# Four sums from GpSimd to VectorE, x loaded plainly for three row blocks, and one sum of weights made in DRAM

## The chip, the cores and the metric

The kernel runs on one core of a Trainium2 chip. The metric is the device time of one execution in microseconds (us); lower is better. Before the change the median of 3 runs was 624.9 us (624.47 to 625.27). The engines are called as the profile calls them: PE is TensorE's matrix product, PEld its loading of weights, DVE VectorE, ACT ScalarE, POOL GpSimd, SP the engine that only issues DMAs. DMAs issued by SP and by GpSimd share 16 DMA engines; only GpSimd's can add to what stands at the destination (accumulate).

## The reference: one decoder layer

For x of 512 rows and 1024 columns:

```python
h = x @ w_in                                  # ua, va, za, q, k, v, zb, ga, gb
ya = gelu(ua) * spatial(layer_norm(gelu(va))) * silu(za)      # branch A
yb = rms_norm(diff_attention(q, k, v)) * silu(zb)             # branch B
merged = sigmoid(ga) * (ya @ w_branch_a) + sigmoid(gb) * (yb @ w_branch_b)
mix_out = merged @ w_out
ple = sigmoid(x @ w_ple_gate) * (p @ w_ple)   # the embedding and its gate
x = layer_norm(ALPHA * x + mix_out + ple)     # ALPHA = 2 ** 0.25
```

All of it is float32.

## The kernel before

**Products.** Every float32 operand is split into a high half (a copy rounded by ScalarE: `wh`, `xh`, `xsh`) and a low half (the difference, a subtraction by VectorE: `wl`, `xl`, `xsl`). A product is three matmuls, high x high, high x low and low x high (`three`). The products of the embedding's gate and of branches A and B, like several before them, are *quads*: a product of two matrices cut into 2 x 2 blocks is made of seven block products instead of eight, as in Strassen's scheme. A quad needs sums of blocks of the left operand (for branch B: of `yb`; for branch A: of `ya`, which lies in the tile `ua`) and sums of blocks of the weights. It runs in seven steps. Each step has two units of weights of 128 x 1024 and 24 matmuls of 128 x 512, so a quad has 168.

**Weights.** A unit is loaded into a buffer `wr`, cut into halves, and used. Sums of weight blocks come in two ways. In the first (`follow`), GpSimd issues an accumulating DMA that adds the next block to the buffer as soon as VectorE has cut it (`wr<-in_w` on POOL). A chain of steps then shares a buffer, and each addition must land before ScalarE can cut the next unit. In the second (`make_sums`, tables `READY_MADE` and `PART_READY`), the sum is made in DRAM ahead of time: SP copies a block into `ws_...`, GpSimd adds another to it, and the step loads the finished sum like any other unit. `PART_READY` says which of the four sums are made so for each quad. From the gates on, eight buffers take the units in order; SP loads the next as soon as a buffer is free.

**Order.** All of the program is one list in order. `later(n, fn)` puts a piece of work n matmuls behind the present one; numbers like `YB_S2` or `GATES` are such distances from the start of a stage. This sets the order on each engine's queue. When an instruction then runs is up to its queue and its semaphores. SP's and GpSimd's queues are in order, too: a DMA that waits holds up all behind it.

**The stages that the change touches**, with their times in the profiled execution: the quad of the embedding's gate (433.5 to 477.5 us), the small product of p (to 488.7), branch B's quad (to 530.2), branch A's quad (to 572.7), and the output product (to 618.5). During the gate's quad the sums of `yb` for branch B's quad and two of those of `ya` are made. `combine` does it: with one number, VectorE makes the sum in one instruction of 128 x 4 x 256; with a pair of numbers, GpSimd makes it in two of half the size. In the gate's quad GpSimd makes four sums in eight instructions (L1235): `YB_S2` and `YB_N4` of `yb`, `YA_S1` and `YA_S3` of `ya`.

**The residual sum.** `embed` multiplies p's product by the gate and by 1/ALPHA into `base`. Then `residue` adds x to `base` by an accumulating DMA, one per block of 128 rows (L1287). In the output stage `fill` has ScalarE copy `base` times ALPHA into a PSUM bank (L1366), and the output product adds to that bank. So the bank ends as ALPHA x + ple + mix_out. VectorE takes statistics from the bank (`stats`, L1374) and normalises it (`last_norm`: L1380 for each bank, then L1384), and SP stores the block. The last block is done in three pieces instead of two.

**Gates.** The sigmoids of ga and gb were stored to DRAM. `load_gates` brings them back, two blocks at a time, into two places of the tile `gates` in turn.

Of the kernel before, what the change touches and what calls it, by code (L numbers as in the profile page):

```python
# [13 lines left out]
F32 = mybir.dt.float32  # L14
# [16 lines left out]
ALPHA = 2.0 ** 0.25  # L31
# [28 lines left out]
SILU = (20,)  # L60
CENTRE = (12, 24)
SPATIAL = (390, 32)
READY_MADE = {'va': (2, 6, 50, 32, 140, 174, 260, 314), 'wb': (162, 290, 170, 318, 356, 470), 'zq': (320, 430, 434, 538), 'ga': (540, 566), 'gb': (752, 786), 'pg': (612, 745)}
APART = 12
TABLES = (12, 40, 84)
TURN_K = (14, 18, 22, 24, 31, 36, 42)
# [25 lines left out]
FILL = ((14, 0, 1), (20, 2, 0), (24, 1, 1), (30, 3, 0), (136, 2, 1), (160, 3, 1), (164, 3, 2))  # L92
RETIRE = 8


# [40 lines left out]

READY = ("11", "21", 0, "22", 1, 2, 3)

PART_READY = {'zq': (0, 2), 'ga': (2,), 'gb': (2,), 'wb': (0, 1, 2), 'pg': (2,)}
KINDS = 'ycyyyyy'  # L140

MAKING = ((0, "begin", "11"), (2, "begin", "22"), (0, "add", "12"), (2, "add", "12"),
# [104 lines left out]
def hybrid_layer(ctx: ExitStack, tc: tile.TileContext, a, out: bass.AP):  # L247
    nc = tc.nc
    pe, dve, act, pool, sp = nc.tensor, nc.vector, nc.scalar, nc.gpsimd, nc.sync
# [5 lines left out]
    big = ctx.enter_context(tc.tile_pool(name="big", bufs=1))  # L255
# [6 lines left out]
    def pp():  # L262
        return pbank("pp", 3)
# [232 lines left out]
    def ask_xr(k):  # L496
# [14 lines left out]
                       base=0, pattern=[[-1, P]], channel_multiplier=1)  # L511
# [5 lines left out]
    cs = rp.tile([P, T], F32, name="cs")  # L517
# [132 lines left out]
    def quad(name, left, banks, place, done):  # L650

        X, Y, Z = banks
        if name == "zq":
            X, Y, Z = ([bank[:, :(2 - t) * 2 * P] for t, bank in enumerate(two)] for two in banks)
        kept = {}

        def keep(key, bank):
            kept[key] = tmp[0](key[0])[:, :bank.shape[-1]]  # L660
            act.activation(kept[key], bank, AF.Copy)  # L661

        def block(c, t, first, second, op, spare):
            z = place(c, t)
            z = spare if z is None else z
            dve.tensor_tensor(out=z, in0=first, in1=second, op=op)
            later(8 if name in SIGMOIDS else 2, done, c, t, z, z)

        goes_on = name in GOES_ON

        def after1(t):
            if goes_on:
                act.activation(X[t], Y[t], AF.Copy)
# [333 lines left out]
    sums.clear()  # L1007
    for name, at in READY_MADE.items():
        make_sums(name, at)
# [106 lines left out]
    va = post.tile([P, NT, D], F32, name="va", tag="V")  # L1116
# [142 lines left out]
    base = post.tile([P, NT, D], F32, name="base", tag="V")  # L1259
# [21 lines left out]

    def embed(c, t, bank):
        z = base[:, t, c * T:(c + 1) * T]
        dve.scalar_tensor_tensor(out=z, in0=bank, scalar=1.0 / ALPHA, in1=z, op0=OP.mult, op1=OP.mult)

    def residue(t):
        pool.dma_start(out=base[:, t, :], in_=a["x"][t * P:(t + 1) * P, :], accum_op=OP.add)  # L1287

    tx = pbank("tx", 1)
    banks = other_banks(), [tx, pp(), pp(), pp()]  # L1290
# [20 lines left out]
    pairs_of_gates = late.tile([P, 2, 2, T], F32, name="gates", tag="R")  # L1311

    def load_gates(name, c, t, i):
        two = pairs_of_gates[:, i]
        gate[name, c, t], gate[name, c, t + 1] = two[:, 0, :], two[:, 1, :]
        sp.dma_start(out=two, in_=gates[name][t:t + 2, c].rearrange("t p n -> p t n"))

    order = [(n, c, t) for n in ("gb", "ga") for c, t in ((0, 0), (1, 0), (1, 2), (0, 2))]
    for i, (n, what) in enumerate(zip(GATES, order)):
        later(n, load_gates, *what, i % 2)  # L1320
# [7 lines left out]
    for t, n in enumerate(RESIDUE):  # L1328
        later(n, residue, t)
    quad("wb", operands(xh, xl, ys, 0), pairs(True), place_b, mb_done)  # L1330

    norm_last = []
# [4 lines left out]

    later(LAST_NORM[0], load_last, "ln_g", "g")
    later(LAST_NORM[1], load_last, "ln_b", "b")

# [17 lines left out]
    last_columns = [[(0, T), (T, D)] for _ in range(NT - 1)] + [[(0, T), (T, T + T // 2), (T + T // 2, D)]]  # L1358
    held = {}

    def fill(t, i):
        c0, c1 = last_columns[t][i]
        bank = (pbank("sc", 2) if (t < 2 and i == 0) or (t >= 2 and i == 1) else
                pbank("tx", 1) if t == 2 else pp())
        held[t, i] = bank[:, :c1 - c0]
        act.activation(held[t, i], base[:, t, c0:c1], AF.Copy, scale=ALPHA)  # L1366

    for t in range(2):
        later(FIRST_FILL[t], fill, t, 0)
    quad("wa", of_ya, pairs(False), lambda c, t: None, merge)  # L1370


    def stats(t, piece, bank):
        dve.bn_stats(out=zst[t][:, piece, :], in_=bank)  # L1374

    def last_norm(t, cuts):
        mv, rs = rstd_of(zst[t])
        lg, lb = norm_last
        for i, cs in enumerate(slice(*c) for c in last_columns[t]):
            dve.scalar_tensor_tensor(out=base[:, t, cs], in0=held[t, i], scalar=mv[:, 0:1], in1=lg[:, cs],  # L1380
                                     op0=OP.subtract, op1=OP.mult)
# [86 lines left out]
```

## Time and profile before

| what | us |
|---|---|
| median of 3 runs | 624.9 |
| the profiled execution's own time | 627.2 |
| its span, first to last instruction | 625.5 |
| TensorE busy | 609.7 (97%) |
| VectorE busy | 465.1 (74%) |
| ScalarE busy | 341.6 (55%) |
| GpSimd busy | 133.8 (21%) |
| mean granted TensorE clock | 0.994 |

DMA moves 138.52 MB, 221 GB/s in the mean. A row of a timeline gives start and length of an instruction in us, its engine, its line, what it writes and reads, and in brackets how long the engine was idle before it and what ended the wait. A start that comes before the end of the row above shows pipelining. In a row of a window, the figure behind each engine is its busy time and the number of instructions; then come the granted clock, the mean busy share of the 16 DMA engines, and GB/s.

### The profile page before, as it was taken

What the parts mean: (1) busy time and instruction counts of PE and PEld (TensorE: products, weight loads), DVE (VectorE), ACT (ScalarE), POOL (GpSimd) and SP (SyncE); (2) the same over time, 40 slices, a digit from 0 to 9 for tenths busy, and PEclk for the clock granted to TensorE, in tenths of its full rate; (3) what the DMA queues carried; (4) which work ended last, traced back from release to release, by engine and by line L of the source; (5) the groups of instructions that cost most, each with busy time, mean ns of one, the idle gap of its engine ahead of it and who ended that gap; (6) DMA issues with size and microseconds to landing.
All of it is one profiled execution on the core that took longest, in us unless ns stands there. A gap on an engine that the chain in (4) does not pass through costs nothing.

```text
span 625.5 us, 8563 instructions
## 1 busy us (share of the span) xinstructions
PE 609.7 (97%) x3012; PEld 510.9 (82%) x3012; DVE 465.1 (74%) x769; ACT 341.6 (55%) x537; POOL 133.8 (21%) x144
## 2 busy tenths in 40 slices
PE   9999999999999999999999999999979998999995
PEld 6888888888888888888899888888858876787885
DVE  6995687878788775657578886677987686769465
ACT  6556664645644754578565656536745454545310
POOL 1234021332431630220102221141540111120000
PEclk9999999999999999999999999999999999999998
DMA  8689899678797696768989898968856887996002
GB/s 304 216 240 187 256 296 286 222 192 280 264 256 270 198 313 181 199 157 289 285 297 224 221 226 242 262 151 237 250 139 197 221 238 224 251 224 225 3 34 102
DMA packets 45631, 138.52 MB, mean 221 GB/s; under 512 B 6036, under 2 KB 7188, under 8 KB 45268
## 3 DMA queue, kind: packets, MB, share of 16 engines
q1 hardware_dynamic: 35092, 102.71, 45.9%
q0 software_dynamic: 9920, 34.87, 30.5%
q8 instruction: 24, 0.39, 0.3%
q10 hardware_dynamic: 576, 0.39, 0.2%
q14 instruction: 19, 0.16, 0.1%
HBM read 118.95 MB, written 30.54 MB: 239 GB/s over the span
## 4 chain that ended last, share of the span: by engine, by line
PE 84%; issue 5%; DMA 5%; DVE 4%; ACT 1%; POOL 0%; DVEq 0%; POOLq 0%; ACTq 0%; SPq 0%
PE ps_pp L281 50%; PE ps_sc L281 15%; PE ps_tx L281 7%; DMA wr<-in_w 3%; PE ps_sc L802 3%; PE ps_po L847 3%; DMA gates<-gate_gb 2%; PE ps_tr L836 1%; DVE wl L413 1%; PE ps_po L281 1%; PE ps_tr L281 1%; DVE xsl L1228 1%; PE ps_po L485 1%; PE ps_tr L1173 1%; PE ps_po L1173 1%
## 5 line engine op out<-in xcount | busy, mean ns | idle before, releaser
L413 DVE TENSOR_TENSOR wl<-wr,wh 128x1024 fp32r<-128x1024 f32 (+1 forms) x143 | 181.3, 1276 | 46.4 <-ACT wh L410 46.0
L410 ACT ACTIVATE wh<-wr 128x1024 fp32r<-128x1024 f32 (+1 forms) x143 | 146.1, 1032 | 73.9 <-DMA wr<-in_w 18.6
L281 PE MATMUL ps_pp<-xh,wh 128*128 128x512 f32 (+1 forms) x276 | 109.8, 399 | 0.0
L281 PE MATMUL ps_pp<-xl,wh 128*128 128x512 f32 (+1 forms) x276 | 107.3, 389 | 0.0
L281 PE MATMUL ps_pp<-xh,wl 128*128 128x512 f32 (+1 forms) x276 | 105.6, 383 | 0.0
L385 POOL DMA_DIRECT2D wr<-in_w x34 | 29.8, 876 | 150.4 <-DVE wl L413 148.1
L815 ACT ACTIVATE p<-p,sth 128x128 f32<-128x128 f32 (+3 forms) x64 | 35.5, 556 | 46.6 <-DVE sth L813 46.5
L281 PEld LDWEIGHTS ps_pp<-xh,wh 128*128 128x128 f32 x276 | 52.5, 190 | 8.6 <-ACT wh L307 0.5
L281 PEld LDWEIGHTS ps_pp<-xh,wl 128*128 128x128 f32 x276 | 52.2, 189 | 8.8
L281 PEld LDWEIGHTS ps_pp<-xl,wh 128*128 128x128 f32 x276 | 52.2, 189 | 8.2 <-DVE xl L308 0.4
L281 PE MATMUL ps_pp<-wh,xh 128*128 128x512 f32 (+1 forms) x144 | 55.3, 384 | 1.2 <-ACT wh L410 1.2
L281 PE MATMUL ps_pp<-wl,xh 128*128 128x512 f32 (+1 forms) x144 | 55.4, 385 | 0.8 <-DVE wl L413 0.8
L281 PE MATMUL ps_pp<-wh,xl 128*128 128x512 f32 (+1 forms) x144 | 55.4, 384 | 0.0
L747 POOL TENSOR_TENSOR hl<-m,hl 128x512 fp32r<-128x512 f32 x16 | 25.1, 1606 | 54.7 <-ACT hl L742 54.7
L809 DVE CUSTOM_DVE_ANT_0 p<-ps_sc,mask 128x128 f32<-128x128 f32 (+3 forms) x64 | 30.9, 483 | 6.4 <-PE ps_sc L802 6.3
L281 PE MATMUL ps_sc<-wl,xsh 128*128 128x512 f32 x88 | 34.7, 394 | 1.0 <-DVE wl L413 1.0
L281 PE MATMUL ps_sc<-wh,xsh 128*128 128x512 f32 x88 | 34.4, 390 | 0.0
L281 PE MATMUL ps_sc<-wh,xsl 128*128 128x512 f32 x88 | 34.3, 390 | 0.0
L281 PE MATMUL ps_pp<-wl,xsh 128*128 128x512 f32 x80 | 32.2, 403 | 2.0 <-DVE wl L413 2.0
L281 PE MATMUL ps_pp<-wh,xsh 128*128 128x512 f32 x80 | 32.0, 400 | 1.3 <-ACT s L661 1.3
L281 PEld LDWEIGHTS ps_pp<-wh,xh 128*128 128x128 f32 x144 | 27.1, 188 | 6.8 <-ACT wh L410 1.7
L281 PEld LDWEIGHTS ps_pp<-wl,xh 128*128 128x128 f32 x144 | 27.1, 188 | 6.3 <-DVE wl L413 1.1
(317 smaller groups left out, 1286.4 us busy)
## 6 DMA issues: line engine op xcount, KB each, us to landing
wr<-in_w SPq DMA_DIRECT2D x81, 512.0 KB, 4.7
wr<-in_w POOLq DMA_DIRECT2D x30, 512.0 KB, 6.6
k<-hl SPq DMA_DIRECT2D x16, 256.0 KB, 5.8
q<-hl SPq DMA_DIRECT2D x16, 256.0 KB, 4.2
ws_va<-in_w POOLq DMA_DIRECT2D x8, 512.0 KB, 10.3
wr<-ws_va SPq DMA_DIRECT2D x8, 512.0 KB, 4.5
wa<-in_w POOLq DMA_DIRECT2D x6, 512.0 KB, 7.4
kx<-hl SPq DMA_DIRECT2D x12, 256.0 KB, 5.8
```

The source lines that it names most:

```text
L281: pe.matmul(ps, s, m, start=start, stop=stop, skip_group_check=read_within)
L385: pool.dma_start(out=raw[u][:, :n], in_=weights(STEPS[FOLLOWS[u]][1], n), accum_op=OP.add)
L410: act.activation(h, raw[u][:, :width(STEPS[u][0])], AF.Copy)
L413: dve.tensor_tensor(out=l, in0=raw[u][:, :width(STEPS[u][0])], in1=h.bitcast(F32), op=OP.subtract)
L485: pe.matmul(idle, zeros[:, :P], zeros, start=True, stop=True)
L747: pool.tensor_tensor(out=hl[:, 3 - j, :], in0=m[2 * j], in1=hl[:, j, :].bitcast(F32), op=OP.subtract)
L802: pe.matmul(sc[m][:, :n], q[:, m, i * P:(i + 1) * P], kk[:, m, :n], start=o == 0, stop=o == 1)
L809: dve.tensor_tensor_reduce(out=pr[m][:, :n], in0=sc[m][:, :n], in1=mask[:, T - n:], scale=-(DK ** -0.5), scalar=3e38, op0=OP.add, op1=OP.m ...
L815: act.activation(pr[m][:, :n], pr[m][:, :n], AF.Exp, bias=st[:, m:m + 1], scale=-1.0, accum_out=st[:, 2 + m:3 + m])
L836: pe.transpose(tr[:, j * P:(j + 1) * P], ad[:, j * P:(j + 1) * P], ident)
L847: pe.matmul(po[:, i * P:(i + 1) * P], at[:, j * P:(j + 1) * P], v[:, j, h * P:(h + 1) * P], start=j == 0, stop=j == i)
L1173: pe.matmul(sa[:, t * P:(t + 1) * P], va[:, t, g * P:(g + 1) * P], aux[0][:, 0, g, :], start=True, stop=True)
```

## The change

**Sums.** `YB_S2`, `YB_N4`, `YA_S1` and `YA_S3` get one number each instead of a pair, so VectorE makes them, one instruction each. The first two stay in the gate's quad; the two of `ya` move to 186 and 222 matmuls from the quad's start, which is in p's product and at the head of branch B's quad. `YA_N4` and two other distances in branch B's quad move a little.

**x.** For row blocks 0 to 2 `base` keeps ple alone. Their blocks of x are loaded plainly by SP into a new tile `rows`, which takes the place of `ua` (ya) once that is used up. They go behind all weights (`RESIDUE`, now counted from the start of branch A's quad). `stats` then has VectorE make ALPHA x rows + bank into `base` before it takes the statistics, and `last_norm` reads `base` once instead of two banks. The last block keeps the accumulating DMA, later than before.

**Weights.** One of the four sums of branch A's weights is made in DRAM during the gate's quad: SP copies two units, GpSimd adds two to them. Step 6 of branch A's quad loads that sum, and its two additions into SBUF go.

**Gate loads.** The last of the eight goes into the unused fourth part of `rows`, so it needs no place of the tile `gates`.

```diff
-READY_MADE = {..., 'pg': (612, 745)}
+READY_MADE = {..., 'pg': (612, 745), 'wa': (1500, 1570)}
-YB11, YB12, YB_S2, YB_N4, YB_SUMS = 25, 49, (34, 46), (58, 70), (75, 101, 124, 226)
-YA22, YA_S1, YA_S3 = 36, (84, 96), (108, 120)
-YA11, YA12, YA_S2, YA_N4, YA_SUMS = 26, 50, 54, 64, (19, 76, 172, 196)
-GATES = (2, 14, 64, 142, 158, 192, 234, 308)
+YB11, YB12, YB_S2, YB_N4, YB_SUMS = 25, 49, 40, 64, (75, 101, 124, 226)
+YA22, YA_S1, YA_S3 = 36, 186, 222
+YA11, YA12, YA_S2, YA_N4, YA_SUMS = 26, 50, 54, 92, (19, 80, 172, 196)
+GATES = (2, 14, 64, 142, 158, 192, 240, 280)
-LAST_NORM = (172, 184)
+LAST_NORM = (214, 224)
-RESIDUE = (10, 34, 58, 82)
+RESIDUE = (176, 190, 204, 164)
-FILL = ((14, 0, 1), (20, 2, 0), (24, 1, 1), (30, 3, 0), (136, 2, 1), (160, 3, 1), (164, 3, 2))
+FILL = ((14, 0, 1), (20, 2, 0), (24, 1, 1), (44, 3, 0), (110, 2, 1), (124, 3, 1), (150, 3, 2))
-PART_READY = {..., 'pg': (2,)}
+PART_READY = {..., 'pg': (2,), 'wa': (2,)}
     def embed(c, t, bank):
         z = base[:, t, c * T:(c + 1) * T]
-        dve.scalar_tensor_tensor(out=z, in0=bank, scalar=1.0 / ALPHA, in1=z, op0=OP.mult, op1=OP.mult)
+        scale = 1.0 if t < NT - 1 else 1.0 / ALPHA
+        dve.scalar_tensor_tensor(out=z, in0=bank, scalar=scale, in1=z, op0=OP.mult, op1=OP.mult)
+    def rows(t):
+        if not spare:
+            spare.append(big.tile([P, NT, D], F32, name="rows", tag="U"))
+        return spare[0][:, t, :]
     def residue(t):
-        pool.dma_start(out=base[:, t, :], in_=a["x"][t * P:(t + 1) * P, :], accum_op=OP.add)
+        x = a["x"][t * P:(t + 1) * P, :]
+        if t == NT - 1:
+            pool.dma_start(out=base[:, t, :], in_=x, accum_op=OP.add)
+        else:
+            x_rows[t] = rows(t)
+            sp.dma_start(out=x_rows[t], in_=x)
-        two = pairs_of_gates[:, i]
+        two = pairs_of_gates[:, i] if i < 2 else rows(NT - 1).rearrange("p (e n) -> p e n", e=2)
-        act.activation(held[t, i], base[:, t, c0:c1], AF.Copy, scale=ALPHA)
+        act.activation(held[t, i], base[:, t, c0:c1], AF.Copy, scale=1.0 if t < NT - 1 else ALPHA)
     def stats(t, piece, bank):
+        if t < NT - 1:
+            z = base[:, t, piece * T:(piece + 1) * T]
+            dve.scalar_tensor_tensor(out=z, in0=x_rows[t][:, piece * T:(piece + 1) * T], scalar=ALPHA, in1=bank,
+                                     op0=OP.mult, op1=OP.add)
+            bank = z
         dve.bn_stats(out=zst[t][:, piece, :], in_=bank)
```

In `last_norm` the loop over banks is left for the last block; the others run it once, over `base`.

How it moves instructions: TensorE's queue is the same in both kernels, row by row. The first place is VectorE's queue in the second and third step of the gate's quad. `y` and `ua` are branch A's spatial gating, `yab` a part of ya, `phl` p. Before:

```order
L413 TENSOR_TENSOR wl<-wr_4062,wh 128x1024
L1228 TENSOR_TENSOR yab<-ua,yag 128x1024
L413 TENSOR_TENSOR wl<-wr_4169,wh 128x1024
L1228 TENSOR_TENSOR xl<-yb,xh 128x4x256
L308 TENSOR_TENSOR phl<-pt,phl 128x512
L413 TENSOR_TENSOR wl<-wr_4202,wh 128x1024
L308 TENSOR_TENSOR phl<-pt,phl 128x512
```

After the change:

```order
L413 TENSOR_TENSOR wl<-wr_4063,wh 128x1024
L1235 TENSOR_TENSOR yb<-yb 128x4x256
L1228 TENSOR_TENSOR yab<-ua,yag 128x1024
L413 TENSOR_TENSOR wl<-wr_4170,wh 128x1024
L1228 TENSOR_TENSOR xl<-yb,xh 128x4x256
L308 TENSOR_TENSOR phl<-pt,phl 128x512
L413 TENSOR_TENSOR wl<-wr_4203,wh 128x1024
L1235 TENSOR_TENSOR yb<-yb 128x4x256
L308 TENSOR_TENSOR phl<-pt,phl 128x512
```

Two sums of `yb` now stand among the low halves there.

The second place is GpSimd's queue from the gate's quad into branch B's. Before:

```order
L385 DMA wr_3988<-in_w 128x1024
L1235 TENSOR_TENSOR yb<-yb 128x2x256
L385 DMA wr_4062<-in_w 128x1024
L1235 TENSOR_TENSOR yb<-yb 128x2x256 x3
L385 DMA wr_3988<-in_w 128x1024
L1235 TENSOR_TENSOR ua<-ua 128x2x256
L385 DMA wr_4062<-in_w 128x1024
L1235 TENSOR_TENSOR ua<-ua 128x2x256 x3
L1287 DMA base<-in_x 128x1024 x3
L385 DMA wr_4642<-in_w 128x1024
L1287 DMA base<-in_x 128x1024
L385 DMA wr_4676<-in_w 128x1024
```

After the change:

```order
L385 DMA wr_3989<-in_w 128x1024
L385 DMA wr_4063<-in_w 128x1024
L342 DMA ws_wa<-in_w 128x1024 x2
L385 DMA wr_4641<-in_w 128x1024
L385 DMA wr_4676<-in_w 128x1024
```

All eight sums and the four additions of x are gone from between the weight additions, and the two additions in DRAM have come in. The last addition of x now follows the last weight addition of branch A.

The third place is VectorE's queue at the end, from the second statistics of row block 2. Before:

```order
L1374 BN_STATS vst<-ps_sc 128x6
L1143 BN_AGGR mv<-vst 128x2
L1144 TENSOR_SCALAR mv<-mv 128x1
L1380 SCALAR_TENSOR_TENSOR base<-ps_tx,mv,ln_g 128x512
L1380 SCALAR_TENSOR_TENSOR base<-ps_sc,mv,ln_g 128x512
L1384 SCALAR_TENSOR_TENSOR base<-base,rs,ln_b 128x1024
```

After the change:

```order
L1389 SCALAR_TENSOR_TENSOR base<-rows,ps_sc 128x512
L1392 BN_STATS vst<-base 128x6
L1143 BN_AGGR mv<-vst 128x2
L1144 TENSOR_SCALAR mv<-mv 128x1
L1402 SCALAR_TENSOR_TENSOR base<-base,mv,ln_g 128x1024
L1406 SCALAR_TENSOR_TENSOR base<-base,rs,ln_b 128x1024
```

The sum with x stands ahead of the statistics, and one operation over the whole block takes the place of two.

More of the change, by code (lines that the diff above doesn't have):

```diff
@@ L62 @@
 SPATIAL = (390, 32)
-READY_MADE = {'va': (2, 6, 50, 32, 140, 174, 260, 314), 'wb': (162, 290, 170, 318, 356, 470), 'zq': (320, 430, 434, 538), 'ga': (540, 566), 'gb': (752, 786), 'pg': (612, 745)}
+READY_MADE = {'va': (2, 6, 50, 32, 140, 174, 260, 314), 'wb': (162, 290, 170, 318, 356, 470), 'zq': (320, 430, 434, 538), 'ga': (540, 566), 'gb': (752, 786), 'pg': (612, 745), 'wa': (1500, 1570)}
 APART = 12
@@ L137 @@
 READY = ("11", "21", 0, "22", 1, 2, 3)
-PART_READY = {'zq': (0, 2), 'ga': (2,), 'gb': (2,), 'wb': (0, 1, 2), 'pg': (2,)}
+PART_READY = {'zq': (0, 2), 'ga': (2,), 'gb': (2,), 'wb': (0, 1, 2), 'pg': (2,), 'wa': (2,)}
 KINDS = 'ycyyyyy'
@@ L1283, in embed @@
         z = base[:, t, c * T:(c + 1) * T]
-        dve.scalar_tensor_tensor(out=z, in0=bank, scalar=1.0 / ALPHA, in1=z, op0=OP.mult, op1=OP.mult)
-    def residue(t):
-        pool.dma_start(out=base[:, t, :], in_=a["x"][t * P:(t + 1) * P, :], accum_op=OP.add)
+        scale = 1.0 if t < NT - 1 else 1.0 / ALPHA
+        dve.scalar_tensor_tensor(out=z, in0=bank, scalar=scale, in1=z, op0=OP.mult, op1=OP.mult)
+    x_rows, spare = {}, []
+    def rows(t):
+        if not spare:
+            spare.append(big.tile([P, NT, D], F32, name="rows", tag="U"))
+        return spare[0][:, t, :]
+    def residue(t):
+        x = a["x"][t * P:(t + 1) * P, :]
[4 more added lines that the diff above has]
+            sp.dma_start(out=x_rows[t], in_=x)
     tx = pbank("tx", 1)
@@ L1319, in hybrid_layer @@
     for i, (n, what) in enumerate(zip(GATES, order)):
-        later(n, load_gates, *what, i % 2)
+        later(n, load_gates, *what, i % 2 if i < 7 else 2)
     split_quarter(YA_SUMS[0], ya22, natural(1, 1))
@@ L1327, in hybrid_layer @@
         split_quarter(n, source, slot(c))
-    for t, n in enumerate(RESIDUE):
-        later(n, residue, t)
     quad("wb", operands(xh, xl, ys, 0), pairs(True), place_b, mb_done)
@@ L1365, in fill @@
         held[t, i] = bank[:, :c1 - c0]
-        act.activation(held[t, i], base[:, t, c0:c1], AF.Copy, scale=ALPHA)
+        act.activation(held[t, i], base[:, t, c0:c1], AF.Copy, scale=1.0 if t < NT - 1 else ALPHA)
     for t in range(2):
         later(FIRST_FILL[t], fill, t, 0)
+    for t, n in enumerate(RESIDUE):
+        later(n, residue, t)
     quad("wa", of_ya, pairs(False), lambda c, t: None, merge)
     def stats(t, piece, bank):
+        if t < NT - 1:
[3 more added lines that the diff above has]
+            bank = z
         dve.bn_stats(out=zst[t][:, piece, :], in_=bank)
@@ L1378, in last_norm @@
         lg, lb = norm_last
-        for i, cs in enumerate(slice(*c) for c in last_columns[t]):
-            dve.scalar_tensor_tensor(out=base[:, t, cs], in0=held[t, i], scalar=mv[:, 0:1], in1=lg[:, cs],
+        if t < NT - 1:
+            first = [(base[:, t, :], slice(0, D))]
+        else:
+            first = [(held[t, i], slice(*c)) for i, c in enumerate(last_columns[t])]
+        for source, cs in first:
+            dve.scalar_tensor_tensor(out=base[:, t, cs], in0=source, scalar=mv[:, 0:1], in1=lg[:, cs],
                                      op0=OP.subtract, op1=OP.mult)
```

## The prediction

> **What bounds the kernel now.** I read the page's shares first, then the windows by stage, then TensorE's own rows for each gap, and last the rows of the engine named behind a gap.
>
> ```profile
> span 625.5 us, 8563 instructions
> core 0: us, PE busy (x) PEld busy (x) DVE busy (x) ACT busy (x) POOL busy (x), PEclk, DMA share, GB/s
> 433.50:455.20 21.70, 21.70 (x101) 18.14 (x100) 18.69 (x16) 16.00 (x20) 9.29 (x8) 1.00 0.84 224
> 455.20:471.90 16.70, 13.44 (x50) 9.96 (x49) 14.57 (x10) 7.98 (x11) 5.87 (x5) 0.90 0.62 155
> 477.70:488.70 11.00, 11.00 (x49) 8.92 (x48) 7.77 (x11) 3.40 (x5) 1.84 (x3) 1.00 0.51 152
> 488.70:530.20 41.50, 38.47 (x166) 30.62 (x165) 30.22 (x31) 20.81 (x24) 4.14 (x5) 1.00 0.86 242
> 530.20:572.70 42.50, 41.33 (x189) 33.60 (x188) 31.83 (x38) 22.13 (x29) 6.31 (x8) 1.00 0.91 229
> 572.70:618.50 45.80, 45.74 (x233) 38.66 (x231) 27.44 (x41) 11.80 (x17) 1.66 (x3) 1.00 0.19 68
> ```
>
> TensorE sets the end, and the change leaves its instructions and their order alone. So it can win only what TensorE loses in gaps and at a low clock. Two of these windows are the embedding gate (433.5 to 477.5), then come the small product with p, branch B's product (from 488.7), branch A's (from 530.2) and the output. In them TensorE is short of its window in four: 3.26, 3.03, 1.17 and 0.06 us. Only the first of these has a clock below 1.00. Here are all its gaps, and first the pace without any (six matmuls in 1.36 us, 0.227 each):
>
> ```profile
> 394.03 0.39 PE L281 MATMUL ps_tx<-wh,xh 128*128 128x512 f32 x1
> ...
> 395.39 0.39 PE L281 MATMUL ps_pp<-wh,xh 128*128 128x512 f32 x1
> ...
> 455.23 0.39 PE L281 MATMUL ps_pp<-wh,xsh 128*128 128x512 f32 x1
> ...
> 457.51 0.50 PE L281 MATMUL ps_pp<-wl,xsh 128*128 128x512 f32 x1 [0.53 <-DVE wl L413]
> 457.85 0.40 PE L281 MATMUL ps_pp<-wh,xsl 128*128 128x512 f32 x1
> ...
> 464.74 0.50 PE L281 MATMUL ps_pp<-wl,xsh 128*128 128x512 f32 x1 [1.45 <-DVE wl L413]
> ...
> 467.43 0.64 PE L281 MATMUL ps_pp<-wh,xsh 128*128 128x512 f32 x1 [1.27 <-ACT s L661]
> 467.87 0.63 PE L281 MATMUL ps_pp<-wl,xsh 128*128 128x512 f32 x1
> ...
> 471.88 0.40 PE L281 MATMUL ps_pp<-wh,xh 128*128 128x512 f32 x1
> ...
> 501.64 0.50 PE L281 MATMUL ps_sc<-wl,xsh 128*128 128x512 f32 x1 [0.52 <-DVE wl L413]
> 507.92 0.50 PE L281 MATMUL ps_sc<-wl,xsh 128*128 128x512 f32 x1 [0.51 <-DVE wl L413]
> 525.55 0.51 PE L281 MATMUL ps_pp<-wh,xh 128*128 128x512 f32 x1 [1.25 <-ACT wh L410]
> 526.82 0.51 PE L281 MATMUL ps_pp<-wl,xh 128*128 128x512 f32 x1 [0.76 <-DVE wl L413]
> 539.85 0.50 PE L281 MATMUL ps_tx<-wh,xh 128*128 128x512 f32 x1 [0.72 <-ACT ps_tx L673]
> 566.01 0.50 PE L281 MATMUL ps_pp<-wh,yag 128*128 128x512 f32 x1 [0.45 <-DVE s L666]
> ```
>
> From 455.23 to 471.88 stand 48 matmuls (steps 5 and 6 of the quad's seven). At pace they take 48 x 0.227 = 10.88 us; they took 16.65. The gate loses **5.77 us** there: 3.25 of waiting and 2.52 of slow matmuls. A restart costs 0.11, as the spacing of 0.34 behind 457.51 shows; with two of these off, 2.3 us are the slow clock's behind the third gap, where the spacing is 0.44. Each gap outside the gate costs its idle time and a restart. Branch B loses 0.52 + 0.51 + 1.25 + 0.76 + 4 x 0.11 = **3.48**, branch A 0.72 + 0.45 + 2 x 0.11 = **1.39**. That makes 10.64 us in all, and no gain from TensorE's gaps can be larger.
>
> **The sums that move from GpSimd to VectorE.** The gaps in the gate wait for VectorE's low halves wl. These are VectorE's rows there, with GpSimd's and the price of one whole sum on VectorE:
>
> ```profile
> 444.85 2.18 DVE L413 TENSOR_TENSOR wl<-wr,wh 128x1024 fp32r<-128x1024 f32 x1 [0.20 <-ACT wh L410]
> 448.69 2.32 DVE L413 TENSOR_TENSOR wl<-wr,wh 128x1024 fp32r<-128x1024 f32 x1
> 450.93 1.78 DVE L308 TENSOR_TENSOR phl<-pt,phl 128x512 fp32r<-128x512 f32 x1
> 453.77 1.21 DVE L1228 TENSOR_TENSOR xsl<-yb,xsh 128x1024 fp32r<-128x1024 f32 x1
> 454.91 3.68 DVE L413 TENSOR_TENSOR wl<-wr,wh 128x1024 fp32r<-128x1024 f32 x2
> 458.51 5.04 DVE L1228 TENSOR_TENSOR xsl<-yb,xsh 128x1024 fp32r<-128x1024 f32 x1
> 458.37 4.08 POOL L1235 TENSOR_TENSOR ua<-ua 128x512 f32<-128x512 f32 x3
> 413.46 4.50 DVE L413 TENSOR_TENSOR wl<-wr,wh 128x1024 fp32r<-128x1024 f32 x1 [2.37 <-ACT wh L410]
> 412.81 4.06 POOL L1235 TENSOR_TENSOR yb<-yb 128x512 f32<-128x512 f32 x3
> L1235 DVE TENSOR_TENSOR ua<-ua 128x1024 f32<-128x1024 f32 x2 | 2.4, 1217 | 0.0
> ```
>
> The same subtraction of 128x1024 takes 1.21 us at 453.77 and 5.04 at 458.51. The second starts 0.14 us after three GpSimd sums that last 4.08 together, and ends just behind them. It happens a stage earlier too (4.50 beside 4.06), where VectorE had room and TensorE no gap. So VectorE stands still while GpSimd adds. Five of the stretched rows above (444.85, 448.69, 450.93, 454.91, 458.51) took 15.0 us; at 1.22, 1.22, 0.68, 2 x 1.22 and 1.22 they would take 6.8. The change takes 8.2 us of standing still from VectorE and adds two sums at 1.22, so VectorE is 5.8 us lighter in the gate: 18.69 + 14.57 - 5.8 = 27.5 us busy in 32.6 at TensorE's pace, 84%. The bounds of this term are 0, if something else stretches those rows, and 5.77. I take **-5.3**, close to the upper end because the two engines' rows match twice; I leave one gap like the first, since the added sums stand ahead of the same low halves.
>
> The other two sums, of ya, now run in the product with p and at the head of branch B, 1.22 us each. Cover: VectorE is busy 7.77 of 11.0 us in the one and 30.22 of 41.5 in the other, and branch B's first bank was read out 5 us before TensorE writes it. Without cover each costs 1.2. The last sum (yb's turn of 64 to 92 for ya) is only moved down. I cost these at 0.
>
> **x no longer added by DMA ahead of branch B.** Each accumulating transfer is dear, which the queues and two rows tell:
>
> ```profile
> q1 hardware_dynamic: 35092, 102.71, 45.9%
> q0 software_dynamic: 9920, 34.87, 30.5%
> L1287 POOL DMA_DIRECT2D base<-in_x x4: 875/882/893, 485.5 to 511.0; - x4
> 499.76 0.69 DVE L1309 TENSOR_TENSOR mb<-ps_pp,gates 128x512 f32<-128x512 f32 x1 [1.64 <-DMA gates<-gate_gb]
> 524.45 2.95 ACT L410 ACTIVATE wh<-wr 128x1024 fp32r<-128x1024 f32 x3 [5.36 <-DMA wr<-in_w]
> ```
>
> Plain transfers run at 102.71 MB / (0.459 x 625.5 us) = 358 GB/s, 1.46 us of all 16 engines for 512 KB. Accumulating ones run at 183, 2.87 us. Before, four of these for x were issued from 485.5 to 511.0: 11.5 us of transfer at the head of a stage whose DMA share is 0.86. The gate load that VectorE waited for at 499.76 travels among them; the weights that ScalarE waited 5.36 us for stand on SP behind the time of the last. Taking away 2.87 us ahead of those weights is more than the 2.01 us of idle TensorE there. Bounds: 0 to 3.48. I take **-3.5**, since the traffic goes from both places. Three plain loads now stand on SP behind the last weight load, about where the output stage begins (572.7, share 0.19). They are first read after that stage's first 48 matmuls, 10.9 us later, and take 3 x 1.46 = 4.4. The addition that is left stands on GpSimd's queue behind the last weight addition, so within branch A, and its reader, the seed of the last block's bank, comes 44 matmuls into the output, 10 us. Both cost 0; without that cover a late row costs VectorE, and the weights behind it, its own 1.46.
>
> **One sum of branch A's weights made in DRAM.** Two accumulations into SBUF (2 x 2.87) become two plain loads (2 x 1.46) in branch A, but x's fourth addition (2.87) comes to its end, so its traffic is about level. One wait fewer in a row of four additions is left. Bounds 0 to 1.39; I take **-0.7**, the middle, having no row nearer to one end. What is added earlier, in the gate, is two copies in DRAM and two additions: at least 2 x 1.46 + 2 x 2.87 = 8.7 us of transfers.
>
> ```profile
> 450.00:480.00 30.00, 26.74 (x108) 20.94 (x107) 24.82 (x19) 16.89 (x21) 9.09 (x7) 0.94 0.58 161
> ```
>
> The room there is 0.42 x 30 = 12.6 us, less the 5.3 that the stage gets shorter: 7.3. So 1.4 us do not fit and push the weights behind them. On SP the two copies stand ahead of the loads of the gate's last and branch B's first weights. Bounds: 0, as the next stage has a share of 0.51, and 8.7. I take **+1.2**, nearer the lower end since 7.3 of the 8.7 have a place.
>
> **The end.** Three blocks get a multiply-add from PSUM and x ahead of each statistic, and one wide operation in place of two:
>
> ```profile
> 618.48 0.43 DVE L1374 BATCH_NORM_STATS2 vst<-ps_pp 128x6 f32<-128x256 f32 x1 [1.57 <-PE ps_pp L281]
> ```
>
> A multiplication of PSUM with SBUF took 0.69 at 499.76; I price the multiply-add by it. The last block's chain is unchanged, and VectorE waits 1.57 us for TensorE before its last statistic, so 0.69 for the third block is hidden. Without that cover it would cost 0.7. I take 0.
>
> **The sum** is -5.3 - 3.5 - 0.7 + 1.2 = -8.3 us. The profiled execution took 627.2 us (1.7 outside its span), 2.3 above the median of 624.9. Taken from the median: **616.6 us**.
>
> **Rivals.** *Only the gate gains* (24%). Branch B's gaps are then due to the weights' own additions, which stay. For it: with the shift the same requests crowd together again. Against it: x's four. 624.9 - 5.3 = 619.6.
>
> *The slow clock is not the gaps' doing* (5%). The clock falls after three gaps of at most 1.45 us and costs 2.3. If that drop has its own cause, it stays: 616.6 + 2.3 = 618.9. The Trainium skill (TensorE: Matmul & The Clock Gate, "What's actually happening") has the clock halve only after an idle window of about 3.4 us; no gap here is that long, so by it this rival would hold. The trace speaks against it, since in these windows the clock is below 1.00 only behind the gaps.
>
> *Nothing moves* (7%). The stretched rows are not GpSimd's doing, or another wait stands behind each gap: 624.9. Against it stand the two matching pairs; for it only that both engines were also sharing the time with accumulating transfers.
>
> *Slower* (8%), by one mechanism: the DRAM copies hold up the gate's last weights and branch B's first. If the full 8.7 us come on the path, the gate's gain and branch B's are eaten: 624.9 - 5.3 + 8.7 = 628.3, and with another clock drop of 2.3 about 631. It decides from the point at which the weights come more than 5.3 us late. For it: the share was 0.84 in the stretch before, and SP's order puts the copies ahead of three loads. Against it: 0.58 over the 30 us that follow.
>
> **How the numbers follow.** My forecast has 56%, with 614.3 (all 10.64 gained) to 618.5 as its own range. The range **614.2 to 621.5** takes in the gate alone with a spill of 1.9 and leaves out the last two rivals, 15%, and little below. A measurement of this kernel can tell 0.2%, 1.25 us, from no change. Faster: 56 + 24 + 5 and 1 of the 7, 86%; same 6%; slower 8%.
>
> **What would show it.** The gate should last 38 to 39 us from its first matmul, with a clock of 1.00 throughout and no low half over 1.3 us; if stretched rows remain without GpSimd sums, the first term falls. In branch B the gate load should come before VectorE asks, and ScalarE's 5.36 us should be gone; if not, the first rival holds. ScalarE or VectorE waiting for the gate's last weights, or for branch B's first, would be the spill, and more than 5 us of it makes the forecast wrong. Behind 572 VectorE should wait for no row of x.

## The result, and the profile after

The changed kernel takes **615.57 us** (median; 615.15 to 616.51) against 624.93 (624.47 to 625.27) of the kernel before in the same comparison: ratio 0.9853, 95% interval 0.9836 to 0.987, so 9.4 us faster. Its profiled execution took 615.15 us, that of before 627.2. These two traces differ by 12.1 us, more than the medians, since before's profiled execution lay above its median; the account below shows most of why. One execution of those reported below, of the kernel without the four sums, was a slow one of 1990.55 us and is left out of the figures.

From the page of the changed kernel, its span, its busy shares and the two DMA queues that move nearly all bytes (packets, MB, share of 16 engines):

```profile
span 613.4 us, 8568 instructions
PE 605.1 (99%) x3012; PEld 510.1 (83%) x3012; DVE 464.5 (76%) x776; ACT 342.3 (56%) x537; POOL 121.5 (20%) x133
...
q1 hardware_dynamic: 35876, 106.38, 48.8%
q0 software_dynamic: 9488, 33.30, 29.9%
```

TensorE is at work 99% of the span. The accumulating queue moves 1.57 MB less (34.87 before), and the plain one 3.67 MB more.

The windows of the changed kernel, for the gate's quad in two parts, p's product, branch B and branch A:

```profile
core 0: us, PE busy (x) PEld busy (x) DVE busy (x) ACT busy (x) POOL busy (x), PEclk, DMA share, GB/s
433.10:454.80 21.70, 21.70 (x101) 18.12 (x100) 17.95 (x18) 16.26 (x20) 3.12 (x4) 1.00 0.96 271
454.80:471.50 16.70, 16.70 (x76) 13.80 (x75) 12.17 (x13) 12.01 (x16) 2.00 (x3) 1.00 1.01 267
471.50:482.60 11.10, 11.10 (x50) 8.99 (x49) 8.91 (x12) 3.50 (x5) 0.00 (x0) 1.00 0.48 176
482.60:520.90 38.30, 38.30 (x171) 31.71 (x170) 31.42 (x33) 21.85 (x25) 3.40 (x4) 1.00 0.77 224
520.90:560.70 39.80, 39.80 (x185) 32.93 (x183) 32.62 (x38) 21.60 (x28) 4.49 (x6) 1.00 0.95 252
```

In every window TensorE's busy time equals the window's length and the clock is 1.00. In before 3.26 us were missing in the gate's second part, 3.03 in branch B and 1.17 in branch A, and the clock was 0.90 in the first of these. What TensorE still waits for in the whole of the changed kernel is one entry (total, times, longest), at the program's start, which before has too:

```profile
PE ps_po L485 <- DVE zeros L482: 1.3, 1, 1.3
```

VectorE's low halves and sums in the gate, and the two sums of `ya` behind it:

```profile
442.45 1.22 DVE L1235 TENSOR_TENSOR yb<-yb 128x1024 f32<-128x1024 f32 x1
448.75 1.22 DVE L1235 TENSOR_TENSOR yb<-yb 128x1024 f32<-128x1024 f32 x1
...
455.95 1.22 DVE L1228 TENSOR_TENSOR xsl<-yb,xsh 128x1024 fp32r<-128x1024 f32 x1
...
475.93 1.22 DVE L1235 TENSOR_TENSOR ua<-ua 128x1024 f32<-128x1024 f32 x1
...
483.16 1.22 DVE L1235 TENSOR_TENSOR ua<-ua 128x1024 f32<-128x1024 f32 x1
```

The subtraction that took 5.04 us beside GpSimd's sums (`xsl<-yb,xsh`) takes 1.22, as does each new sum. In branch B the two waits that the prediction pointed to now read, on VectorE and on ScalarE:

```profile
491.91 0.68 DVE L1322 TENSOR_TENSOR mb<-ps_pp,gates 128x512 f32<-128x512 f32 x1
...
513.48 2.96 ACT L410 ACTIVATE wh<-wr 128x1024 fp32r<-128x1024 f32 x3 [2.18 <-DMA wr<-in_w]
```

The wait for the gate load is gone. ScalarE's wait for weights fell from 5.36 to 2.18 us: the prediction had it gone, but TensorE doesn't feel what is left.

### The profile page after: what moved, and what is told of

Read it like the earlier page. It is cut to its first block, busy times and chain, and to the rows that moved or that the text cites. A ratio compares the mean times of both kernels' runs of the same rounds, so it can differ in the third digit from the quotient of the medians.

```text
span 613.4 us, 8568 instructions
## 1 busy us (share of the span) xinstructions
PE 605.1 (99%) x3012; PEld 510.1 (83%) x3012; DVE 464.5 (76%) x776; ACT 342.3 (56%) x537; POOL 121.5 (20%) x133
## 4 chain that ended last, share of the span: by engine, by line
PE 99%; DVE 0%; DVEq 0%; issue 0%
PE ps_pp L281 58%; PE ps_sc L281 19%; PE ps_tx L281 9%; PE ps_sc L802 3%; PE ps_po L847 3%; PE ps_tr L836 1%; PE ps_po L281 1%; PE ps_tr L281 1%; PE ps_po L485 1%; PE ps_tr L1173 1%; PE ps_po L1173 1%; PE ps_tx L886 0%; PE ps_po L1360 0%; PE ps_tr L1360 0%; DVE base L1402 0%; DVEq L1486 0%
## 5 line engine op out<-in xcount | busy, mean ns | idle before, releaser
L413 DVE TENSOR_TENSOR wl<-wr,wh 128x1024 fp32r<-128x1024 f32 (+1 forms) x143 | 177.8, 1250 | 39.3 <-ACT wh L410 39.0
L385 POOL DMA_DIRECT2D wr<-in_w x32 | 27.7, 876 | 181.0 <-DVE wl L413 127.0
L281 PEld LDWEIGHTS ps_pp<-wh,xl 128*128 128x128 f32 x144 | 27.1, 188 | 5.2
L281 PE MATMUL ps_pp<-wh,xsl 128*128 128x512 f32 x80 | 31.2, 390 | 0.0
```

Of the source, the lines that this page charges most:

```text
L281: pe.matmul(ps, s, m, start=start, stop=stop, skip_group_check=read_within)
L385: pool.dma_start(out=raw[u][:, :n], in_=weights(STEPS[FOLLOWS[u]][1], n), accum_op=OP.add)
L413: dve.tensor_tensor(out=l, in0=raw[u][:, :width(STEPS[u][0])], in1=h.bitcast(F32), op=OP.subtract)
```

## The experiments

Theory A, in the texts on record, is the prediction's: GpSimd's sums stop VectorE and so open the gate's gaps; x's accumulating transfers crowd the weights and open branch B's. What stands against it is told there, run by run. Each comparison below has its own runs of before beside it (medians 624.1, 624.4 and 625.0).

### Each part alone and each part left out

*Before, with only the four sums on VectorE:*

```diff
-YB11, YB12, YB_S2, YB_N4, YB_SUMS = 25, 49, (34, 46), (58, 70), (75, 101, 124, 226)
-YA22, YA_S1, YA_S3 = 36, (84, 96), (108, 120)
+YB11, YB12, YB_S2, YB_N4, YB_SUMS = 25, 49, 40, 64, (75, 101, 124, 226)
+YA22, YA_S1, YA_S3 = 36, 186, 222
```

> The kernel before with one part of the change: VectorE makes the four sums (YB_S2 = 40, YB_N4 = 64, YA_S1 = 186, YA_S3 = 222). x and the weights are as before. Theory A (three parts, each with its own gaps): only the gate's gaps go, 3.5 us if the slow clock of the profile is not in every execution, 5.8 with it: 619.1 to 621.4 us, and the profile keeps the gaps in branch B and A, about 5.7 us in all. Theory B (one cause: the gate's late finish crowds the DMAs of the branches): nearly all goes, 615.6 to 617, and TensorE has no gap left. Theory C (the sums on VectorE win nothing by themselves): 624.9.

Measured 619.58 us (617.61 to 620.79), ratio 0.9924, interval 0.9897 to 0.9951: -4.5 us. What TensorE waits for in it (the start's 1.3 left out):

```profile
PE ps_sc L281 <- DVE wl L413: 1.0, 2, 0.5
PE ps_pp L281 <- DVE s L666: 0.7, 1, 0.7
PE ps_pp L281 <- DVE wl L413: 0.4, 1, 0.4
PE ps_tx L281 <- ACT s L661: 0.4, 1, 0.4
PE ps_pp L281 <- ACT s L661: 0.2, 1, 0.2
```

None of these lies in the gate's quad; the first, second, third and last are in branches B and A, 2.3 us in all, where the text before the run expected about 5.7. So the gate's gaps are the sums' doing, and the branches' are not.

*The change, with the four sums back on GpSimd* (the same two lines, the other way round):

> The changed kernel with the four sums back on GpSimd at their old places; x and the weights stay changed. Theory A: the gate's gaps are back and only they: 615.6 + 3.5 to 5.8 = 619.1 to 621.4 us. Theory B: the branches' gaps are back as well: 624 to 625. Theory C: 615.6.

Measured 621.16 us (619.88 to 622.08), ratio 0.9943, interval 0.9926 to 0.996. TensorE's waits:

```profile
PE ps_pp L281 <- DVE wl L413: 2.2, 2, 1.5
PE ps_pp L281 <- ACT s L661: 1.3, 1, 1.3
...
PE ps_pp L281 <- DVE base L666: 0.6, 1, 0.6
PE ps_tx L281 <- ACT s L661: 0.4, 1, 0.4
```

The mirror image: the first three rows are the gate's, the last lies ahead of it (at 424.09), and in branches B and A there is none.

*The change without the sum of weights in DRAM:*

```diff
-READY_MADE = {..., 'pg': (612, 745), 'wa': (1500, 1570)}
+READY_MADE = {..., 'pg': (612, 745)}
-PART_READY = {..., 'pg': (2,), 'wa': (2,)}
+PART_READY = {..., 'pg': (2,)}
```

> The changed kernel without the sum of branch A's weights in DRAM: step 6 of branch A's quad gets its two additions into SBUF back, and the four transfers in the gate's quad go. Theory A: branch A's gaps are back, up to 1.7 us: 616.3 to 617.3 us; if the transfers in the gate's quad cost 1.2 as I took, that comes off: 615 to 616. Theory B: 615.6, no gap. If x's addition at the end of branch A now crowds with the four weight additions: over 617.3.

Measured 614.64 us (614.55 to 615.47), ratio 0.9852, interval 0.9826 to 0.9878, and no gap in any stage. Since the first comparison had no run of the whole change beside it, both were run together once more:

> The changed kernel again, beside the next run on the same chip: 615 to 616.5 us, and no gap on TensorE from the gate to the end.

> The changed kernel without the sum of branch A's weights in DRAM, again (614.64 us in the first run, on another chip than the changed kernel's). If that part wins branch A's wait, 0.5 to 1.7 us above the changed kernel; if it is worth nothing once x is out of the way, within 0.5 of it; if its four transfers in the gate's quad cost something, 0.5 to 1.2 below it, as the first run suggests.

The whole change 615.42 (614.82 to 616.09), ratio 0.9848, interval 0.9822 to 0.9873; without the DRAM sum 615.03 (614.67 to 615.36), ratio 0.9842, interval 0.9817 to 0.9867. The ranges overlap: that part is worth nothing that can be measured here, and no cost of its transfers can be told from nothing either. They are seen in the window of the gate's last part, here of the kernel without them, to be held against 1.01 above:

```profile
454.80:471.50 16.70, 16.70 (x75) 13.82 (x74) 12.17 (x13) 11.94 (x16) 0.00 (x0) 1.00 0.77 228
```

*x's part alone* (the change without the DRAM sum and with the sums back on GpSimd):

> The kernel before with x's part alone (with the gate loads and fills that belong to it): the four sums stay on GpSimd, no sum of branch A's weights in DRAM. Theory A: branch B's gaps go, 3.5 to 4 us, the gate's stay: 621 to 621.5 us. Theory B: no gain, 624.9, with the gaps in branch B still there. Theory C (x was the whole of it): 615.6 to 617.

Measured 621.21 us (619.96 to 623.17), ratio 0.9959, interval 0.9941 to 0.9976: -2.9 us. All its waits are the gate's:

```profile
PE ps_pp L281 <- DVE wl L413: 2.1, 2, 1.5
PE ps_pp L281 <- ACT s L661: 1.3, 1, 1.3
```

With x plain for three blocks, branch A has no gap either, although branch A's weights are added by DMA as before. This part changes two things at once: x's transfers are plain in place of accumulating, and they stand behind the weights in place of ahead of them. No run takes the two apart.

### What the sums themselves cost, and why GpSimd stops VectorE

*Before, with the four sums left out* (their four calls of `combine` removed, so only its time means anything):

> The kernel before with the four sums (YB_S2, YB_N4, YA_S1, YA_S3) left out, so that neither GpSimd nor VectorE makes them; branches A and B then use unsummed blocks, and only the time counts. Set beside the run with the sums on VectorE (619.6 us, 4.5 below the kernel before): if VectorE makes them for nothing, as I costed, this run lies within 1 us of it, 4 to 5.5 below before, and the gate has no gap. If the sums on VectorE cost part of their 4 x 1.22, it lies up to 4.9 us below it. If the gate's gaps are not GpSimd's doing, it equals before.

Measured 618.84 us (618.17 to 619.17), ratio 0.9908, interval 0.9881 to 0.9936, and no gap in the gate. That is 0.7 below the kernel with the sums on VectorE, or 1.0 by the two ratios, each to its own runs of before; the intervals overlap. So of the 4.9 us that four sums take on VectorE, most lies beside TensorE's work, and a cost of about 1 us is neither shown nor ruled out.

*The change, with eight needless additions on GpSimd* where the sums stood:

```diff
+    scratch = base[:, NT - 1, T:]
+    later(30, lambda: pool.memset(scratch, 0.0))
+    def idle_work():
+        pool.tensor_tensor(out=scratch, in0=scratch, in1=scratch, op=OP.add)
+    for n in (34, 46, 58, 70, 84, 96, 108, 120):
+        later(n, idle_work)
```

> The changed kernel with eight needless GpSimd additions of 128x512 put where its eight sums were (they read and write a part of the tile base that is not yet in use). Theory A (a GpSimd instruction that reads SBUF stops VectorE's with two SBUF inputs): VectorE's rows are stretched by about the length of each, the gate's gaps are back, 3.5 to 6 us: 619 to 621.5. Theory D (the gaps came from the waits between these sums and the splits, or from added DMA): 615.6.

*The same with three memsets in place of each addition*, so that GpSimd writes and reads nothing:

```diff
-        pool.tensor_tensor(out=scratch, in0=scratch, in1=scratch, op=OP.add)
+        for _ in range(3):
+            pool.memset(scratch, 0.0)
```

> The same, but each needless addition is three memsets of 128x512, which write SBUF and read nothing. If GpSimd stops VectorE whenever it is at work in SBUF: stretched rows again and 617 to 621.5 us, by how long the memsets are. If only its reads do so, as the Trainium skill has it (SBUF, 'Who interferes with whom': a VectorE instruction with two SBUF inputs contends with a GpSimd instruction that reads SBUF, not with one that only writes it): no stretched row, no gap, 615.6.

With additions 619.85 us (618.8 to 620.8), ratio 0.9925, interval 0.99 to 0.9949; with memsets 616.47 (615.93 to 617.55), ratio 0.9875, interval 0.9843 to 0.9906. GpSimd and VectorE in the gate, first with additions:

```profile
444.24 5.30 POOL L1268 TENSOR_TENSOR base<-base 128x512 f32<-128x512 f32 x3
...
456.15 5.67 POOL L1268 TENSOR_TENSOR base<-base 128x512 f32<-128x512 f32 x1
...
444.38 2.28 DVE L1228 TENSOR_TENSOR yab<-ua,yag 128x1024 fp32r<-128x1024 f32 x1
446.58 2.06 DVE L413 TENSOR_TENSOR wl<-wr,wh 128x1024 fp32r<-128x1024 f32 x1
448.57 2.06 DVE L1228 TENSOR_TENSOR xl<-yb,xh 128x1024 fp32r<-128x1024 f32 x1
```

and with memsets:

```profile
445.59 5.54 POOL L1269 MEMSET base<- 128x512 f32 x9
...
446.93 1.22 DVE L413 TENSOR_TENSOR wl<-wr,wh 128x1024 fp32r<-128x1024 f32 x1
448.07 1.22 DVE L1228 TENSOR_TENSOR xl<-yb,xh 128x1024 fp32r<-128x1024 f32 x1
```

GpSimd is about as long at work in both (17.0 us with the eight additions, 14.8 with the memsets), yet only its additions stretch the same instructions of VectorE (2.06 against 1.22). The additions touch nothing that VectorE uses, so it is not the data. It goes both ways: one addition, the fifth, took 5.67 us (at 456.15), while VectorE ran row on row. The Trainium skill (SBUF — State Buffer, "Who interferes with whom") has it so: a VectorE instruction with two SBUF inputs contends with a GpSimd instruction that reads SBUF, not with one that only writes it, and the one that comes second waits out the other. Both kernels agree with that.

With the additions the gate has gaps again, though not where before has them. These are two; a third, of 0.27, follows at 470.70:

```profile
452.41 0.50 PE L281 MATMUL ps_sc<-wl,xsh 128*128 128x512 f32 x1 [1.19 <-DVE wl L413]
...
468.54 0.50 PE L281 MATMUL ps_pp<-wh,xh 128*128 128x512 f32 x1 [1.10 <-DVE base L666]
```

The third stands behind ScalarE's wait of 3.38 us for weights (468.33). GpSimd issued a weight addition only at 461.77 (456.73 with memsets), behind the addition of 5.67, so a GpSimd that is held up also delays the transfers on its queue. With the memsets the gate has no gap; the kernel's two others (0.83 at 6.66, 0.36 at 424.59) lie ahead of it.

### What x's additions cost, wherever they travel

*The kernel with only the sums moved, and x's four accumulating transfers moved too*, from the start of branch B to the start of branch A:

```diff
-    for t, n in enumerate(RESIDUE):
-        later(n, residue, t)
...
+    for t, n in enumerate(RESIDUE):
+        later(n, residue, t)
     quad("wa", of_ya, pairs(False), lambda c, t: None, merge)
```

> The sums on VectorE, and x still added by four accumulating DMAs, but each a whole quad later: at the distances 10, 34, 58, 82 of branch A's quad instead of branch B's. No sum of branch A's weights in DRAM. Theory A (the four additions delay whatever travels beside them): branch B's gaps (about 1.9 us in the run with the sums alone) go, and branch A's grow from 1.2 to 2 us or more: 618.5 to 621. Theory E (branch B's gaps come from the additions' place behind p's product, and elsewhere they are hidden): 615 to 616.5, as in the changed kernel. If the gaps stay in branch B, it was not x: 619.6.

Measured 624.79 us (623.98 to 627.2), ratio 1.0011, interval 0.9994 to 1.0029: all that the sums had gained is lost. Branch B then has no gap; branch A has two of 0.76 and 0.77, and this between them, on ScalarE and on TensorE:

```profile
552.40 1.06 ACT L410 ACTIVATE wh<-wr 128x1024 fp32r<-128x1024 f32 x1 [3.99 <-DMA wr<-in_w]
...
554.00 0.79 PE L281 MATMUL ps_pp<-wh,xsh 128*128 128x512 f32 x1 [3.44 <-ACT s L661]
...
558.85 0.63 PE L281 MATMUL ps_pp<-wh,xsl 128*128 128x512 f32 x1
```

Its DMA queues between 530 and 560 us, and its DMA issues there (count, KB each, median us to landing):

```profile
q0 software_dynamic: 1363, 4.98, 83.4%
...
wr<-in_w POOLq DMA_DIRECT2D x5, 512.0 KB, 14.5
```

The accumulating queue alone takes 83.4% of all engines' time for 4.98 MB in 30 us, and a weight addition takes 14.5 us to land (7.1 over the whole of the changed kernel). The gap is late weights: TensorE waits for a bank that ScalarE reads out at 553.36, behind the row above. That branch B's gaps went with the transfers is as Theory A has it; but the kernel takes 5.2 us more than the one with only the sums moved, and what branch A would give back was underestimated.

What x's transfers do to others shows in branch B. Here are SP's plain loads of ready sums of its weights, with x's additions beside them (only the sums moved) and with those moved away:

```profile
wr<-ws_wb SPq DMA_DIRECT2D x4, 512.0 KB, 8.9
...
wr<-ws_wb SPq DMA_DIRECT2D x4, 512.0 KB, 3.6
```

They land after 3.6 us in place of 8.9, and the gate loads after 5.5 in place of 10.9 (medians of four). Both are issued by SP, so what slows them is not a place in GpSimd's queue but the traffic beside them, on the same 16 DMA engines.

### Where the time goes in each: an account

*The kernel before, profiled a second time:*

> The kernel before, profiled once more, to see whether the slow clock behind the gate's third gap comes in every execution. If it does: 8 matmuls at half pace again. If it depends on where the gaps fall against something that the program does not set: the same three gaps without slow matmuls, and a time about 2 us lower.

This execution took 624.01 us. Its gate has five gaps, not three: 0.71, 1.47 and 1.26 us where the first profile has its three, and these two:

```profile
451.34 0.50 PE L281 MATMUL ps_sc<-wl,xsh 128*128 128x512 f32 x1 [0.52 <-DVE wl L413]
...
471.27 0.50 PE L281 MATMUL ps_pp<-wh,xh 128*128 128x512 f32 x1 [0.56 <-DVE base L666]
```

Its row of the gap that the first profile has as the third, and the next:

```profile
467.68 0.49 PE L281 MATMUL ps_pp<-wh,xsh 128*128 128x512 f32 x1 [1.26 <-ACT s L661]
468.01 0.39 PE L281 MATMUL ps_pp<-wl,xsh 128*128 128x512 f32 x1
```

The gap is as long as in the first profile (1.27 us there), but the matmuls behind it run at pace. In the first profile eight of them were slow, up to the first of these two rows of it:

```profile
470.86 0.48 PE L281 MATMUL ps_pp<-wh,xsl 128*128 128x512 f32 x1
471.18 0.39 PE L281 MATMUL ps_pp<-wh,xsh 128*128 128x512 f32 x1
```

From 467.43 to 471.18 nine matmuls took 3.75 us in place of 9 x 0.227 = 2.04: 1.7 lost, of which 0.11 is the restart that any gap has. That leaves 1.6. The times agree: of before's 52 runs beside the experiments, the 15 with a mean granted clock under 0.9935 have a median of 625.2, the 28 over 0.9955 of 623.8. A mean clock of 0.995 or less came only with four kernels, and all four have the gate's third gap or the one of 3.44 us: before, the change with the sums on GpSimd, x alone, and x later. The 40 executions of the others all have 0.996 to 0.998.

With that, each profiled execution can be accounted for. A gap costs its idle time, 0.11 for the restart, and 0.16 that a matmul's row (0.39) is longer than the pace (0.227). Slow matmuls are the excess of their spacing, less one restart:

| kernel | profiled execution | waits but the start's | gaps x 0.27 | slow matmuls | what is left |
|---|---|---|---|---|---|
| before | 627.2 | 7.5 | 9: 2.4 | 1.6 | 615.7 |
| before, second profile | 624.0 | 6.5 | 9: 2.4 | 0 | 615.1 |
| sums alone | 619.8 | 2.6 | 6: 1.6 | 0 | 615.5 |
| sums left out | 619.2 | 2.1 | 4: 1.1 | 0 | 616.0 |
| change, sums on GpSimd | 621.8 | 4.4 | 5: 1.4 | 0 | 616.1 |
| x alone | 621.3 | 3.4 | 3: 0.8 | 1.6 | 615.5 |
| change with additions | 618.8 | 2.6 | 3: 0.8 | 0 | 615.4 |
| change with memsets | 616.8 | 1.2 | 2: 0.5 | 0 | 615.1 |
| sums alone, x later | 624.8 | 5.2 | 4: 1.1 | 2.5 | 616.0 |
| the change | 615.15 | 0 | 0 | 0 | 615.15 |
| without the DRAM sum | 614.64 | 0 | 0 | 0 | 614.64 |

Whatever the kernel, 614.6 to 616.1 us are left. So the differences are TensorE's gaps and its clock, to within about 1.5 us, and nothing is left for the changed kernel to gain in this way but the start's 1.3.

## Why the prediction was right, and where its terms were off

The forecast was 616.6 us, with 614.3 to 618.5 as its own range; 615.57 lies in it. By its steps:

**The gate's sums, -5.3.** Right in mechanism, shown by the kernels with additions and with memsets. Alone the part gave -4.5; on top of x it gave 621.21 - 614.64 = -6.6. The gate lasts 39.0 us (432.21 to 471.20) where 38 to 39 were said, without the one gap that the prediction left standing. Mis-sized was the slow clock in it: 1.6 us, not 2.3, and not in every execution. The prediction took all of the 2.52 us that the waits in brackets didn't cover, less two restarts, for slow matmuls; 3 x 0.16 of it was the modelled end of the rows, another 0.11 the third restart, and the last 0.1 spacings of 0.23 to 0.24 between the gaps.

**The ceiling of 10.64 us** fell for the same reason. With 0.27 a gap in place of 0.11, before's profiled execution lost 7.5 + 2.4 + 1.6 = 11.5 us.

**x no longer added by DMA, -3.5.** Right for branch B. Alone it gave -2.9, on top of the sums 619.58 - 614.64 = -4.9. It was mis-sized in two ways. Branch B's 3.48 was that of one execution: by its second profile before lost 2.3 us there (0.60, 0.53 and 0.33, and 0.27 for each). And x's part also closed branch A's gaps (0.72 and 0.45 in the first profile), which the prediction gave to the weights' own additions: they went with x alone, while those additions stayed. That x's additions opened them, and not the gate loads and fills that x's part moves with it, was not taken apart.

**One sum of weights in DRAM, -0.7 and +1.2.** Both were 0, as far as the overlapping ranges can tell. The gap that the -0.7 was to close had gone with x. The spill is there as traffic (DMA share 1.01 against 0.77 in the gate's last part), but TensorE waited for no weights.

**The added sums of ya and the output stage, 0.** Right: no gap beside the sums, and behind 560 us VectorE waits for no row of x. The cover at the end fell more than was counted, from 1.57 to 0.57 us before the last statistic; how is told below.

**The sum.** Of the terms -5.3 - 3.5 - 0.7 + 1.2 = -8.3, the last two were wrong and cancelled to 0.5. The measured -9.4 is one more than forecast. That it came so near is in part luck: the terms were read from an execution of 627.2 us, and taken from the median. In the second profile, 624.0 us and nearer to the median, the gate lost 5.9 us by its five gaps with no slow clock at all, branch B 2.3 and branch A 0.8 (at the idle time and 0.27 for each gap). The total of 8.9 lies close to the forecast's 8.3, with other parts.

**The rivals.** *Only the gate gains* fell with x's part alone (-2.9). *Nothing moves* and *slower* fell with the result; the copies held up nothing that TensorE waited for. *The slow clock is not the gaps' doing* is refuted as a source of the time: the clock is 1.00 in all windows after and 0.996 or more in every execution of the kernels that have neither the gate's third gap nor that of 3.44 us, and in the stages accounted for slow matmuls were seen only behind gaps, of 1.27 us in two of the kernels profiled, of 3.44 in one. But the same gap of 1.26 also passed without any. What decides between the two stays open. The Trainium skill (TensorE: Matmul & The Clock Gate, "What's actually happening") gives full clock back after a busy window of about 3.4 us. Two slow stretches lasted 3.4 (467.43 to 470.86) and 3.5 us, but the third 5.3 (554.00 to the end of the last slow one). The idle window of the same length that it names for the fall fits the gap of 3.44; behind those of 1.27 the clock fell without it.

**What stays open.** The parts alone give 4.5 + 2.9 = 7.4 us, together 9.5. The account may say where part of it is: with the sums alone the gaps outside the gate cost 4.3 us, in before's second profile 3.0, and the difference lies in branch A and ahead of the gate. But before's first profile has 5.8 there, and the gap ahead of the gate (0.37) also came with the sums on GpSimd (0.36). So such gaps differ from one execution to the next, and one profile of each kernel doesn't show that the sums' gain was given back. Open, too, is whether x's loads help because they are plain or because they stand behind the weights.

## What to carry to other kernels

When TensorE sets the end, list its gaps and price each from start to start of the matmuls at its two sides; the idle time that a profile shows before a row leaves part of the loss out. Work that is moved to a rarely busy engine is not free when both engines read SBUF at once: look for one instruction with two durations. An accumulating transfer took about twice the DMA time of a plain one here (2.87 against 1.46 us for 512 KB, by the means of the two queues), so take accumulating transfers away from where weights are tight, and add on an engine that has room.

## What the runs showed of the hardware that was not expected

GpSimd can be the one that waits, for a thing as small as one number a row. The end of the changed kernel, VectorE's and GpSimd's rows, where `rs` is a power of one column:

```profile
602.48 1.27 DVE L1402 SCALAR_TENSOR_TENSOR base<-base,mv,ln_g 128x1024 f32<-128x1024 f32 x1
604.19 1.28 DVE L1406 SCALAR_TENSOR_TENSOR base<-base,rs,ln_b 128x1024 f32<-128x1024 f32 x1 [0.44 <-POOL rs L1146]
...
606.38 0.43 DVE L1392 BATCH_NORM_STATS2 vst<-ps_pp 128x6 f32<-128x256 f32 x1 [0.57 <-PE ps_pp L281]
...
602.64 1.51 POOL L1146 TENSOR_TENSOR rs<-mv,mhalf 128x1 f32<-128x1 f32 x1 [4.00 <-DVE mv L1144]
607.35 0.55 POOL L1146 TENSOR_TENSOR rs<-mv,mhalf 128x1 f32<-128x1 f32 x1 [3.20 <-DVE mv L1144]
```

and the answering row of before:

```profile
613.94 0.55 POOL L1146 TENSOR_TENSOR rs<-mv,mhalf 128x1 f32<-128x1 f32 x1 [4.89 <-DVE mv L1144]
```

In before, and for the last block after (607.35), VectorE's operation beside it reads a PSUM bank, and `rs` takes 0.55 us. Where the change made that operation one over two SBUF operands (602.48), `rs` takes 1.51 and ends 0.40 behind it, and VectorE waits 0.44 for `rs`. It costs nothing here, as 0.57 us of cover is left. That it is the same contention as in the gate is argued from the rows; no run took it apart.

The other was how much more x's four accumulating transfers, 11.5 us of DMA time by the prediction's rows, cost in a stage with more of their kind. With the sums on VectorE, they cost 4.9 us at the start of branch B (619.58 against 614.64 with x's part) and 10.1 us at the start of branch A (624.79 against 614.64).
